# A decoder block in FP32: five instead of four steps by seven products in FFN blocks 3 to 10, and 28 instead of 20 weight sum sets

## The chip, the cores and the metric

The kernel runs on one core of a Trainium2 chip. The metric is the device time of one execution in microseconds (us), lower is better. The kernel before takes 1686.55 us, the median of three runs (1684.89 to 1690.86).

## The reference

One layer of a decoder block on 256 positions of width 2048, all in float32. Cut to what is computed:

```python
a = rmsnorm(h, norm_mix_pre)
proj = a @ w_in                                    # (2048, 17408)
q_a, k_a, v_a, q_r, f_r, i_r, g_r, gate_a, gate_r = split_columns(proj)
attn = ...       # 3 groups of 8 heads, rotary, dilated windows, outputs mixed by their denominators
r_out = ...      # HGRN2 gated linear recurrence, 8 heads, per-head RMSNorm, times silu(g_r)
y = sigmoid(gate_a) * (attn @ w_attn_branch) + sigmoid(gate_r) * (r_out @ w_hgrn_branch)
h = h + rmsnorm(y @ w_mix_out, norm_mix_post)
a = rmsnorm(h, norm_ffn_pre)
gt, up = jnp.split(a @ w_ffn_gate_up, [D_FF], axis=-1)     # D_FF = 5632
ff = (silu(gt) * up) @ w_ffn_down
h = h + rmsnorm(ff, norm_ffn_post)
```

Nearly all the arithmetic is in the products with the weights, 314 MB of them, each used once.

## The kernel before

**A product in float32.** Weights and activations are split into a high part (ScalarE copies into float32r) and a low part (VectorE subtracts). Each product of a weight tile is three matmuls: high by high, high by low, low by high.

**Items.** The program is one loop over `items` (line 669). An item is a step of a wide block (`steps`) or a chunk of a narrow one (`chunks`). Items 0 to 79 are the ten wide blocks on `w_in`, eight steps each. Items 80 to 175 are the chunks of the query and key blocks (n = 0 to 95), in which the recurrence and the attention run beside the products. Items 176 to 191 are chunks of the gate columns, 192 to 207 of the recurrence's output branch, 208 to 223 of the attention's branch. Items 224 to 239 are the mixing product, then come eleven FFN blocks (gate and up columns together, eight steps each) and two blocks of the down product.

**A wide step** multiplies four weight tiles of 128 x 512 (two row tiles k by two column groups g, 1 MB in all) by both halves of the positions: eight products, 24 matmuls. Where the block's order says so, the same 2 x 2 x 2 product is made **by seven** products (Strassen's scheme as Winograd wrote it), 21 matmuls. This needs sums of the activations (`pair_sums`, kept in `h7` for the FFN) and four sums of the weight tiles. In the orders of lines 39 to 47 each pair is (row pair m, way): 0 is plain, 1 is by seven with the weight sums made by VectorE in the step itself (lines 443 to 449), 2 is by seven with sums made long before and kept in HBM.

**The weight sums made before** come from `weight_sums` (line 296): GpSimd issues DMAs that copy tiles inside HBM and DMAs that add onto them. One set is eight DMAs of 256 KB. The generator goes forward one pass at a time from `ahead_of_time` (line 338): a pass first copies one column of the weights of item i + 3 (`beats`), so it waits until they have landed. A set of 20 jobs takes 184 passes. Before, there is a pass in each odd wide step from item 12 and in every chunk. A way 2 step loads one sum in place of a tile (line 283) and three more, 768 KB, into `sum` (line 336).

**What sets the order.** Each engine works in the order in which the program issues. For item i the loop issues `prepare(i)` (the split of item i + 2, the sums of i + 4, the loads up to three raw buffers beyond, on SP's queue), the matmuls, one pass of each lane (recurrence, attention), the evacuations, and `ahead_of_time`. The raw buffers hold 1 MB each and there are 3; there are 3 buffers for `w` and `wl`, 4 for `dh` and `dl` (two by-seven steps). `gather_first` and `gather_second` (lines 510 to 530) add the seven products' banks together after the last by-seven step of a block. A block's four result banks come from one PSUM pool and its banks of partial products from the other; `flip` says which way round.

**Around the attention.** `evac_rope` (line 920) applies the rotary factors with VectorE. `recurrence` (line 1023) works in six levels, each with matmuls, a predicated copy out of PSUM and three multiplications on VectorE. `attention` (line 948) takes the heads one after the other. All these share a ring of 17 buffers of 512 KB (`fslot`). `make_room` (line 1587) ends that phase at item 210.

Of the kernel before, what the change touches and what calls it, by code (L numbers as in the profile page):

```python
# [14 lines left out]
F32 = mybir.dt.float32  # L15
# [6 lines left out]
P = 128  # L22
# [21 lines left out]
]  # L44
GATE_UP3 = [(3, 0), (4, 0), (0, 2), (5, 0), (1, 1), (6, 0), (2, 2), (7, 0)]
GATE_UP4 = [(4, 0), (5, 0), (0, 2), (6, 0), (1, 1), (2, 2), (3, 1), (7, 0)]
DOWN = [[(m, m in by7) for m in range(KF // 2)] for by7 in (range(4, 20, 3), (2, 4, 7, 10, 13, 16, 18))]

N_F, N_RAW, N_SPLIT, AHEAD, WARM, BRIDGE = 17, 3, 3, 2, 8, 6


# [49 lines left out]
def tile_hybrid_block(ctx: ExitStack, tc: tile.TileContext, t, out):  # L101
# [194 lines left out]
    def weight_sums(jobs):  # L296
# [25 lines left out]
        for at in range(len(jobs) + 3):  # L322
# [5 lines left out]
            yield  # L328
            yield

    def fetch_sums(i):
        if i < len(items) and items[i][0] is steps:
            n = items[i][1]
            if n in pre:
                pre_in[n] = sum_slot()
                nc.sync.dma_start(pre_in[n], pre[n][:, 512:])

    def ahead_of_time(i):

        if back and (items[i][0] is chunks or i % 2):  # L340
            ahead = items[i + 3][0][items[i + 3][1]][2]
            nc.gpsimd.tensor_copy(beats, ahead[:, :1])  # L342
            advance(back)

    def split(i):
# [211 lines left out]
    def pair_sums(src, out, slot, pairs=H7):  # L557

        for m in pairs:
            f = ptile("f").rearrange("p (k t) -> p k t", k=2)  # L560
            x = src.slots[m]
            nc.vector.tensor_add(f, x[:, :, 0, :].bitcast(F32), x[:, :, 1, :].bitcast(F32))
            dst = slot().rearrange("p (z n t) -> p z n t", z=2, n=4)
            yield
            for part in seven_sums(f, dst):
                yield
                part()
            out[m] = sums_of(dst)
            yield
# [95 lines left out]
        return row[:, None, :].to_broadcast([P, n, S])  # L665

    evacs, turns, lanes, queue = deque(), deque(), [deque(), deque()], deque()
    back, turned, hold, gathers = deque(), deque(), [False], []
    ready = set()

    def advance(q):
# [248 lines left out]
    def evac_rope(key, tab, then=None):  # L920

        cos = tabs[:, tab, :]
        sin = tabs[:, tab + 1, :]

        def ev(i, src):
            if i == 0:
                qkT[key] = fslot("qk").rearrange("p (h t) -> p h t", h=4)
            yield
            w = ptile("w").rearrange("p (h t) -> p h t", h=2)
            for o, n in ((0, 64), (64, 0)):  # L930
                nc.scalar.activation(w[o : o + 64], src[n : n + 64], AF.Copy)
            yield
            u = src
            nc.vector.tensor_mul(u, src, by_rows(cos, 2))  # L934
            nc.vector.tensor_mul(w, w, by_rows(sin, 2))  # L935
            nc.vector.tensor_add(
                qkT[key][:, 2 * i : 2 * i + 2, :].rearrange("p h (two j) -> p h two j", two=2),
                u.rearrange("p h (j two) -> p h two j", two=2),
                w.rearrange("p h (j two) -> p h two j", two=2),
            )  # L940
            if i == 1 and then:
                then()
        return ev
# [79 lines left out]
    def recurrence(half):  # L1023
# [61 lines left out]
        for lev, w in enumerate(LEVELS):  # L1085
            rows = P - w if w > 8 else P
            ps = aux() if w > 1 else added(0)
            beat[0] = tick[0]
            for e in range(8) if w > 1 else ():
                es = slice(e * P, (e + 1) * P)  # L1090
                mm(
                    spans(ps[:rows, e * 64 : (e + 1) * 64], w), kk[:, e * P : e * P + rows],
                    spans(q[:, es], 2 * w)[:, :, w:], True, True,
                )
            yield
            if w < 32:
                nc.vector.copy_predicated(
                    at[:rows].rearrange("p (e n w) -> p e n w", e=8, w=2 * w)[:, :, :, w:],
                    lmask[:rows, lev, :].rearrange("p (n w) -> p n w", w=w)[:, None, :, :]
                    .to_broadcast([rows, 8, 64 // w, w]).bitcast(I32),  # L1100
                    ps[:rows].rearrange("p (e n w) -> p e n w", e=8, w=w),
                )
            for n in range(2) if w == 32 else ():
                nc.scalar.activation(
                    at[64 * n : 64 * n + 32].rearrange("p (e n w) -> p e n w", e=8, w=w)[:, :, 2 * n + 1, :],
                    ps[64 * n : 64 * n + 32].rearrange("p (e n w) -> p e n w", e=8, w=w)[:, :, n, :],
                    AF.Copy,
                )
            n = 1024 // (2 * w)
            end = spans(end, 2)  # L1110
            for x, l, r in ((kk, slice(0, w), 1), (q, slice(w, 2 * w), 0)):
                y = spans(x, 2 * w)[:, :, l]
                nc.vector.tensor_mul(y, y, end[:, :, r : r + 1].to_broadcast([P, n, w]))
            new = ends[:, used : used + n]
            used += n
            nc.vector.tensor_mul(new, end[:, :, 0], end[:, :, 1])
            end = new
            if w == 8 and half == 0:
                nc.scalar.preload_act_table_set("natural_log_exp_and_others")
            yield  # L1120
            yield
        qe, ke = (x.rearrange("p (e c t) -> p e c t", e=8, c=2) for x in (q, kk))
        ps = aux()
# [248 lines left out]
    def more_h(c):  # L1372
        if c + 1 < KD // 2:
            transpose_in(h_t, colg[:, 16:32], hT[0], c + 1)
        if c == 3:
            mix_gain(3, 1, wides[last_mix])
            residual_of(6, (0, 1), False)
            residual_of(7, (0, 1), False)
            lanes[0].append(second_norm())
        if c == 4:  # L1380
            lanes[1].append(pair_sums(hT[0], h7, lambda: rslot("so"), range(4)))

    def second_norm():
        ss, s2 = small("ss"), small("s2")
# [202 lines left out]
    def make_room(c):  # L1587
        if c == 2:
            flush(evacs)
            end_phase1()  # L1590

    early = [
# [47 lines left out]
    add_wide_block(w, (0, FF), PLAIN, lambda k: hT[0](k), None, evac_first, True, mid=more_h)  # L1640
    spare = wides[-1], 0
    for j in range(1, 11):
        add_wide_block(w, (512 * j, FF + 512 * j), GATE_UP4 if j > 1 else GATE_UP3, lambda k: hT[0](k),
                       lambda m: h7[m], evac_ffn, j % 2 == 0,
                       pre=begin_wides if j == 1 else None, turn=1)
    for j in range(2):
        add_wide_block(t["w_ffn_down"][0], (1024 * j, 1024 * j + 512), DOWN[j], act,
                       lambda m: a7[m], evac_down, j % 2 == 0, prep=prep_act,
                       pre=begin_down if j == 0 else None, turn=3 if j == 0 else None)

    wides[len(early) - 1].pre = lambda: turned.append(turned_inputs())
    wides[-3].post = lambda c: fetch_act(c // 2) if c in (1, 3) else None
    back.append(
        weight_sums([n for n, (b, i, *_) in enumerate(steps) if b.order[i][1] == 2])
    )

    load_x(0, 0, 256)
    load_wide(0, ((0, (0,)), (0, (1,))))
# [10 lines left out]
    for i in range(len(items)):  # L1669
# [13 lines left out]
            continue  # L1683
        if not (wide and b.mid):
            prepare(i)
        gather_second()
        if i >= len(items) - 3:
            continue
        multiply(i)
        if not fp:  # L1690
            gather_second()
        if b.post:
            b.post(c)
        advance(evacs)
# [77 lines left out]
```

## Time and profile before

| | us |
|---|---|
| median of three runs | 1686.55 |
| profiled execution, its own time | 1685.82 |
| its span, first to last instruction | 1684.0 |
| TensorE busy | 1670.0 |
| VectorE busy | 1374.0 |
| ScalarE busy | 1003.6 |
| GpSimd busy | 207.3 |

Durations of matmuls overlap, so a matmul's rate is read from the chain of waits (so many matmuls in so many us). In a table of windows each engine has its busy time and its instructions; the last two columns are the mean busy share of the 16 DMA engines and what they moved in GB/s. A share of 1.00 means that all of them were busy.

### The profile page before, as it was taken

What the parts mean: (1) busy time and instruction counts of PE and PEld (TensorE: products, weight loads), DVE (VectorE), ACT (ScalarE), POOL (GpSimd) and SP (SyncE); (2) the same over time, 40 slices, a digit from 0 to 9 for tenths busy, and PEclk for the clock granted to TensorE, in tenths of its full rate; (3) what the DMA queues carried; (4) which work ended last, traced back from release to release, by engine and by line L of the source; (5) the groups of instructions that cost most, each with busy time, mean ns of one, the idle gap of its engine ahead of it and who ended that gap; (6) DMA issues with size and microseconds to landing.
All of it is one profiled execution on the core that took longest, in us unless ns stands there. A gap on an engine that the chain in (4) does not pass through costs nothing.

```text
span 1684.0 us, 21755 instructions
## 1 busy us (share of the span) xinstructions
PE 1670.0 (99%) x8023; PEld 1398.8 (83%) x8023; DVE 1374.0 (82%) x1433; ACT 1003.6 (60%) x1077; POOL 207.3 (12%) x358
## 2 busy tenths in 40 slices
PE   9999999999999999999999999999999999999997
PEld 7888888888888888888888888888888888888886
DVE  6988888888786877674568878898888888898987
ACT  6666555555555545555545547666766666665653
POOL 0010101111443333232321000000000000000000
PEclk9999999999999999999999999999999999999999
DMA  8667878789999998989988656998888888888673
GB/s 293 212 215 261 257 247 246 255 258 260 271 251 265 253 249 223 226 227 291 305 215 281 214 173 200 288 272 265 286 272 270 283 263 282 271 279 273 225 266 115
DMA packets 258283, 423.47 MB, mean 251 GB/s; under 512 B 46800, under 2 KB 97152, under 8 KB 258176
## 3 DMA queue, kind: packets, MB, share of 16 engines
q1 hardware_dynamic: 231728, 360.83, 66.8%
q0 software_dynamic: 17984, 41.97, 13.2%
q10 hardware_dynamic: 8464, 19.28, 3.1%
q8 instruction: 63, 1.03, 0.3%
q14 instruction: 44, 0.36, 0.1%
HBM read 397.89 MB, written 58.20 MB: 271 GB/s over the span
## 4 chain that ended last, share of the span: by engine, by line
PE 95%; DVE 2%; DMA 1%; ACT 1%; issue 0%; DVEq 0%; ACTq 0%; SPq 0%
PE acc L138 58%; PE aux L138 36%; DMA raw<-in_w_in 1%; DVE w L380 1%; PE aux L987 0%; ACT w L379 0%; DVE wl L434 0%; PE aux L630 0%; DVE fz L1548 0%; ACT w L432 0%; DVE e L535 0%; ACT junk L1502 0%; PE aux L617 0%; DVE w L935 0%; DVE sum L934 0%
## 5 line engine op out<-in xcount | busy, mean ns | idle before, releaser
L434 DVE TENSOR_TENSOR wl<-raw,w 128x2048 fp32r<-128x2048 f32 (+1 forms) x150 | 327.2, 2188 | 87.8 <-ACT w L432 87.0
L432 ACT ACTIVATE w<-raw 128x2048 fp32r<-128x2048 f32 (+1 forms) x150 | 273.8, 1833 | 110.0 <-PE acc L138 32.8
L380 DVE TENSOR_TENSOR w<-raw,w 128x1024 fp32r<-128x1024 f32 x144 | 175.9, 1222 | 132.4 <-ACT w L379 132.4
L138 PE MATMUL acc<-xT,w 128*128 128x512 f32 (+1 forms) x1536 | 277.0, 339 | 0.2 <-DVE w L380 0.2
L138 PEld LDWEIGHTS acc<-xT,w 128*128 128x128 f32 x1536 | 235.3, 189 | 34.1 <-DVE w L380 0.6
L379 ACT ACTIVATE w<-raw 128x1024 fp32r<-128x1024 f32 x144 | 152.2, 1058 | 158.7 <-PE acc L138 115.7
L454 DVE TENSOR_TENSOR wl<-raw,w 128x2048 fp32r<-128x2048 f32 x83 | 190.0, 2290 | 31.3 <-ACT w L439 20.9
L138 PE MATMUL acc<-w,xT 128*128 128x512 f32 x694 | 207.1, 391 | 0.0
L342 POOL COPY beats<-raw 128x1 f32<-128x1 f32 x185 | 97.6, 528 | 722.9 <-DMA raw<-in_w_in 581.9
L138 PE MATMUL acc<-w,hT 128*128 128x512 f32 x510 | 166.7, 391 | 0.4 <-DVE hT L1302 0.4
L442 ACT ACTIVATE w<-raw 128x1536 fp32r<-128x1536 f32 x63 | 93.9, 1490 | 100.6 <-PE acc L138 40.3
L138 PEld LDWEIGHTS acc<-w,xT 128*128 128x128 f32 x694 | 129.8, 188 | 26.7
L456 DVE TENSOR_TENSOR dl<-sum,dh 128x1536 fp32r<-128x1536 f32 x83 | 145.3, 1751 | 1.7 <-ACT dh L452 1.7
L138 PE MATMUL aux<-w,xT 128*128 128x512 f32 x454 | 144.9, 389 | 0.0
L138 PE MATMUL aux<-w,hT 128*128 128x512 f32 x414 | 134.6, 389 | 0.0
L452 ACT ACTIVATE dh<-sum 128x1536 fp32r<-128x1536 f32 x83 | 123.4, 1487 | 10.7 <-PE acc L138 3.3
L138 PEld LDWEIGHTS acc<-w,hT 128*128 128x128 f32 x510 | 95.7, 188 | 20.5 <-DVE hT L1302 0.9
L138 PEld LDWEIGHTS aux<-w,xT 128*128 128x128 f32 x454 | 85.2, 188 | 17.7
L138 PE MATMUL acc<-wl,hT 128*128 128x512 f32 x255 | 99.3, 389 | 0.0
L138 PE MATMUL acc<-wl,xT 128*128 128x512 f32 x251 | 97.7, 389 | 0.0
L138 PEld LDWEIGHTS aux<-w,hT 128*128 128x128 f32 x414 | 77.7, 188 | 16.1
L138 PE MATMUL acc<-w,a 128*128 128x512 f32 x282 | 89.2, 389 | 0.2 <-DVE e L535 0.2
(282 smaller groups left out, 3029.3 us busy)
## 6 DMA issues: line engine op xcount, KB each, us to landing
raw<-in_w_in SPq DMA_DIRECT2D x270, 512.0 KB, 5.8
raw<-in_w_ffn_gate_up SPq DMA_DIRECT2D x156, 512.0 KB, 5.5
raw<-in_w_ffn_down SPq DMA_DIRECT2D x88, 512.0 KB, 5.4
presum<-in_w_ffn_gate_up POOLq DMA_DIRECT2D x120, 256.0 KB, 7.3
raw<-in_w_mix_out SPq DMA_DIRECT2D x32, 512.0 KB, 5.0
sum<-presum SPq DMA_DIRECT2D x20, 768.0 KB, 6.7
act<-acts SPq DMA_DIRECT2D x22, 512.0 KB, 6.8
presum<-presum POOLq DMA_DIRECT2D x40, 256.0 KB, 6.4
```

The costliest lines, as they stand in the source:

```text
L138: nc.tensor.matmul(ps, lhsT, rhs, start=start, stop=stop, skip_group_check=True)
L342: nc.gpsimd.tensor_copy(beats, ahead[:, :1])
L379: nc.scalar.activation(wh, raw, AF.Copy)
L380: nc.vector.tensor_sub(wl, raw, wh.bitcast(F32))
L432: nc.scalar.activation(hi[:, c], raw[:, c], AF.Copy)
L434: nc.vector.tensor_sub(lo[:, c], raw[:, c], hi[:, c].bitcast(F32))
L442: nc.scalar.activation(hi[:, 512:], raw[:, 512:], AF.Copy)
L452: nc.scalar.activation(high, sums, AF.Copy)
L454: nc.vector.tensor_sub(lo, raw, hi.bitcast(F32))
L456: nc.vector.tensor_sub(low, sums, high.bitcast(F32))
```

## The change

FFN blocks 3 to 10 take a new order, `GATE_UP5`: three plain steps, three of way 2 and two of way 1, where `GATE_UP4` had four, two and two. `pair_sums` makes the activation sums of row pair 4 as well. This asks for 28 sets of weight sums: GpSimd makes the first 20 as before, the other 8 are made by `weight_sums_beside`. It loads four tiles by SP's queue into two ring buffers, lets VectorE add four times and stores the set by ScalarE's queue. Two such generators run, from items 177 and 181, seven passes to a set, one pass per item; `make_room` empties them. GpSimd's passes come in every wide step, in two of three chunks up to n = 127 and in each chunk after it. Moved are: the three multiplications of each recurrence level (ahead of the predicated copy, in a pass of their own), a pass in `evac_rope`, and `gather_second` (directly after the item's matmuls). The two down blocks swap their PSUM pools.

```diff
+GATE_UP5 = [(5, 0), (6, 0), (0, 2), (2, 2), (1, 1), (4, 2), (3, 1), (7, 0)]
+SPARSE = 128
+N_SUMS, BESIDE = 20, 177
...
+    def weight_sums_beside(jobs):
+        for n in jobs:
+            x = [fslot("pre") for _ in range(2)]
+            b, i = steps[n][:2]
+            m = b.order[i][0]
+            r = [x[g][:, c * 512 : (c + 1) * 512] for g, c in ((0, 1), (0, 0), (1, 0), (1, 1))]
+            for q, (g, k) in enumerate(product(range(2), repeat=2)):
+                rows = slice((2 * m + k) * P, (2 * m + k + 1) * P)
+                nc.sync.dma_start(r[q], b.w[rows, b.cols[g] : b.cols[g] + 512])
+            for _ in range(3):
+                yield
+            for to, by in ((2, 0), (0, 1), (1, 2), (3, 1)):
+                nc.vector.tensor_add(r[to], r[to], r[by])
+                if by:
+                    yield
+            pre[n] = dram.tile([P, 2048], F32, name=nm("presum"))
+            for g in range(2):
+                nc.scalar.dma_start(pre[n][:, g * 1024 : (g + 1) * 1024], x[g])
+            yield
...
     def ahead_of_time(i):
-        if back and (items[i][0] is chunks or i % 2):
+        for n, q in enumerate(beside):
+            if i >= BESIDE + 4 * n:
+                advance(q)
+        kind, n = items[i][:2]
+        if back and (kind is steps or n >= SPARSE or n % 3):
             ahead = items[i + 3][0][items[i + 3][1]][2]
-            nc.gpsimd.tensor_copy(beats, ahead[:, :1])
+            nc.gpsimd.tensor_copy(beats, ahead[:, 1023:1024])
             advance(back)
...
     def pair_sums(src, out, slot, pairs=H7):
         for m in pairs:
+            for _ in range(8 if m == 4 else 0):
+                yield
...
     # evac_rope, between the multiplications and the addition
+            if not then:
+                yield
...
     # recurrence, each level: these lines now stand ahead of the predicated copy
+            for x, l, r in ((kk, slice(0, w), 1), (q, slice(w, 2 * w), 0)):
+                y = spans(x, 2 * w)[:, :, l]
+                nc.vector.tensor_mul(y, y, end[:, :, r : r + 1].to_broadcast([P, n, w]))
+            new = ends[:, used : used + n]
+            nc.vector.tensor_mul(new, end[:, :, 0], end[:, :, 1])
+            yield
...
-            lanes[1].append(pair_sums(hT[0], h7, lambda: rslot("so"), range(4)))
+            lanes[1].append(pair_sums(hT[0], h7, lambda: rslot("so"), range(5)))
...
     def make_room(c):
         if c == 2:
             flush(evacs)
+            for q in beside:
+                flush(q)
             end_phase1()
...
-        add_wide_block(w, (512 * j, FF + 512 * j), GATE_UP4 if j > 1 else GATE_UP3, lambda k: hT[0](k),
+        add_wide_block(w, (512 * j, FF + 512 * j), (None, GATE_UP3, GATE_UP4)[j] if j < 3 else GATE_UP5, lambda k: hT[0](k),
...
-                       lambda m: a7[m], evac_down, j % 2 == 0, prep=prep_act,
+                       lambda m: a7[m], evac_down, j % 2 == 1, prep=prep_act,
...
+    back.append(weight_sums(kept[:N_SUMS]))
+    for n, q in enumerate(beside):
+        q.append(weight_sums_beside(kept[N_SUMS + n :: 2]))
...
-        gather_second()
         if i >= len(items) - 3:
             continue
         multiply(i)
-        if not fp:
-            gather_second()
+        gather_second()
```

More of the change, by code (lines that the diff above doesn't have):

```diff
@@ L667, in tile_hybrid_block @@
     evacs, turns, lanes, queue = deque(), deque(), [deque(), deque()], deque()
-    back, turned, hold, gathers = deque(), deque(), [False], []
+    back, beside, turned, hold, gathers = deque(), (deque(), deque()), deque(), [False], []
     ready = set()
@@ L1095, in recurrence @@
             yield
+            n = 1024 // (2 * w)
+            end = spans(end, 2)
+            for x, l, r in ((kk, slice(0, w), 1), (q, slice(w, 2 * w), 0)):
+                y = spans(x, 2 * w)[:, :, l]
+                nc.vector.tensor_mul(y, y, end[:, :, r : r + 1].to_broadcast([P, n, w]))
+            new = ends[:, used : used + n]
+            used += n
+            nc.vector.tensor_mul(new, end[:, :, 0], end[:, :, 1])
+            end = new
+            yield
             if w < 32:
@@ L1108, in recurrence @@
                 )
[L1109 to L1117, printed above, removed]
             if w == 8 and half == 0:
                 nc.scalar.preload_act_table_set("natural_log_exp_and_others")
-            yield
             yield
@@ L1652, in tile_hybrid_block @@
     wides[-3].post = lambda c: fetch_act(c // 2) if c in (1, 3) else None
-    back.append(
-        weight_sums([n for n, (b, i, *_) in enumerate(steps) if b.order[i][1] == 2])
-    )
+    kept = [n for n, (b, i, *_) in enumerate(steps) if b.order[i][1] == 2]
+    back.append(weight_sums(kept[:N_SUMS]))
+    for n, q in enumerate(beside):
+        q.append(weight_sums_beside(kept[N_SUMS + n :: 2]))
     load_x(0, 0, 256)
```

## The prediction, made before the changed kernel was run

> **What bounds the kernel now.** I read the page's first part, then the windows by stage, then the chain of waits.
>
> ```profile
> span 1684.0 us, 21755 instructions
> PE 1670.0 (99%) x8023; PEld 1398.8 (83%) x8023; DVE 1374.0 (82%) x1433; ACT 1003.6 (60%) x1077; POOL 207.3 (12%) x358
> ```
>
> ```profile
> core 0: us, PE busy (x) PEld busy (x) DVE busy (x) ACT busy (x) POOL busy (x), PEclk, DMA share, GB/s
> 67.00:428.00 361.00, 361.00 (x1594) 298.94 (x1593) 310.42 (x241) 209.20 (x172) 43.73 (x63) 1.00 0.79 249
> 428.00:545.00 117.00, 117.00 (x724) 103.37 (x723) 91.56 (x127) 67.31 (x95) 44.59 (x75) 1.00 1.00 259
> 545.00:585.00 40.00, 39.84 (x231) 34.44 (x230) 30.06 (x47) 24.24 (x42) 14.50 (x28) 1.00 1.01 258
> 585.00:610.00 25.00, 22.92 (x139) 20.21 (x138) 19.92 (x28) 11.28 (x17) 9.42 (x17) 0.99 1.02 254
> 610.00:750.00 140.00, 139.82 (x876) 124.20 (x876) 98.12 (x157) 74.30 (x126) 41.21 (x77) 0.99 0.90 226
> 750.00:860.00 110.00, 110.00 (x557) 93.44 (x556) 58.79 (x83) 56.85 (x76) 34.69 (x65) 1.00 1.00 279
> 1117.00:1443.00 326.00, 326.00 (x1440) 270.04 (x1439) 287.74 (x211) 221.23 (x170) 0.00 (x0) 1.00 0.88 274
> ```
>
> TensorE sets the time: it is idle for 14.0 us of 1684.0, and its granted clock is 0.99 to 1.00. So fewer matmuls are worth their full time if nothing else becomes late. What could is to be seen in the last columns. From 428 to 610 us and again from 750 to 860 us the DMA engines are full (share 1.00 to 1.02) and TensorE still hardly waits. In the FFN stretch, which is blocks 3 to 10, VectorE is 88% busy and the DMA engines 88%.
>
> **The matmuls saved.**
>
> ```profile
> 944.41 11.56 PE aux L138 x51
> ```
>
> A matmul takes 11.56 / 51 = 0.227 us in this piece of the chain. A plain step is 24 of them, 5.44 us, one by seven 21, 4.76 us. Eight blocks change one step each: 24 matmuls, **-5.4 us**.
>
> **What the extra step costs in the FFN.** Rows of the FFN stretch alone (groups of instructions, window 1117 to 1443):
>
> ```profile
> L454 DVE TENSOR_TENSOR wl<-raw,w 128x2048 fp32r<-128x2048 f32 x32 | 73.3, 2290 | 25.7 <-ACT w L439 16.0 <-ACT w L450 9.7
> L434 DVE TENSOR_TENSOR wl<-raw,w 128x2048 fp32r<-128x2048 f32 x32 | 72.6, 2287 | 8.1 <-ACT w L432 8.0
> L456 DVE TENSOR_TENSOR dl<-sum,dh 128x1536 fp32r<-128x1536 f32 x32 | 56.0, 1751 | 1.7 <-ACT dh L452 1.7
> L452 ACT ACTIVATE dh<-sum 128x1536 fp32r<-128x1536 f32 x32 | 47.4, 1481 | 6.6 <-PE acc L138 3.3 <-PE aux L138 2.4
> L443 DVE TENSOR_TENSOR sum<-raw 128x1024 f32<-128x1024 f32 x16 | 19.5, 1216 | 0.0
> L448 DVE TENSOR_TENSOR raw<-raw,sum 128x512 f32<-128x512 f32 x16 | 11.1, 692 | 0.5
> ```
>
> A block takes 180 x 0.227 = 40.8 us now and 40.1 us after. VectorE has 287.74 / 8 = 36.0 us of work in it; one `dl` of 1.75 us comes on top: 37.7 of 40.1, 94%. ScalarE goes from 27.7 to 29.1 us. The average fits, but the five by-seven steps now stand in a row. A step of way 2 needs 2.29 + 1.75 = 4.04 us of VectorE, one of way 1 also the three sums (1.22 + 2 x 0.69), 6.6 us: five steps need 3 x 4.04 + 2 x 6.6 = 25.4 us while TensorE takes 5 x 4.76 = 23.8 us. So VectorE loses 1.6 us of its lead over TensorE in them, where before three in a row cost 4.04 + 2 x 6.6 - 3 x 4.76 = 3.0 us after a plain step had given it time (5.44 - 2.29 = 3.2 us). Worse is the buffer: there are four `dh`/`dl`, two steps' worth, so ScalarE's `dh` of step k + 2 can't begin before TensorE ends step k; the rows show such waits already (6.6 us for 32). Behind it in ScalarE's order stand the next high part and the transposed activations. Bounds: nothing, if the lead lasts, and 1 us a block, if each run of five ends with TensorE waiting. I take 0.2 us a block, **+1.6 us**, near the lower end since the average has 2.4 us to spare a block. The load of 768 KB more a block adds about 2.5 us of DMA time (priced below) to 0.88 x 40.8 = 35.9: 38.4 of 40.1 us, covered by the three raw buffers loaded ahead.
>
> `gather_second` comes 1 to 2 us earlier in VectorE's order. There it waits for the seventh product, and behind it waits the low part of the item after next, which needs its `w` buffer from the same step anyway: nothing. Row pair 4's activation sums are fewer than eight VectorE operations of at most 0.7 us each, spread by eight passes: nothing, since their use lies blocks later; uncovered they would be under 5 us once.
>
> **The down blocks' banks.**
>
> ```profile
> 1442.83 0.70 DVE e L535
> 1443.67 22.73 PE acc L138 x99
> ```
>
> The last FFN block and the first down block use the same pool now, so TensorE waits for the addition that frees a bank. The swap takes that away. It can be worth nothing, if TensorE had just come, or the addition's whole 0.70 us; I take the middle, **-0.4 us**.
>
> **Passes and order around the attention.** The page's queues price a DMA:
>
> ```profile
> q1 hardware_dynamic: 231728, 360.83, 66.8%
> q0 software_dynamic: 17984, 41.97, 13.2%
> q10 hardware_dynamic: 8464, 19.28, 3.1%
> ```
>
> Shares are of 1684 us of all 16 engines. SP's queue (q1): 1125 us for 360.83 MB, 3.12 us a MB. ScalarE's (q10): 2.71 us a MB. GpSimd's (q0): 222 us in 184 passes, 1.21 us a pass. Before there are 34 passes up to item 79 and 96 in items 80 to 175; after it is 68 and 64. So 34 x 1.21 = 41 us of DMA time move into 67 to 428 us, whose share rises from 0.79 to 0.90: nothing, covered by the loads ahead; if that cover fails, a few us. And 39 us leave the stretch 428 to 750, whose share falls from about 0.96 to 0.84.
>
> ```profile
> 601.87 1.31 DVE L1097 COPY_PREDICATED at<-lmask,aux 128x512 f32<-128x512 int32 x1
> 602.98 0.72 DVE L1113 TENSOR_TENSOR kk<-kk,f 128x512 f32<-128x512 f32 x1
> 603.62 0.68 DVE L1113 TENSOR_TENSOR q<-q,f 128x512 f32<-128x512 f32 x1
> 604.22 0.68 DVE L1116 TENSOR_TENSOR end<-f 128x512 f32<-128x512 f32 x1
> ```
>
> These four VectorE operations in a row, with the rotary's three ahead, stand before the split at 607 us, and TensorE loses 25.00 - 22.92 = 2.1 us there. The edits put passes between them, and late loads are fewer. I take **-2.2 us**, all idle time of 428 to 610; the bounds are -2.4 and, if the copy that is now later holds its PSUM bank too long, +2.
>
> **The eight sets of `weight_sums_beside`.** They run in items 177 to 210.
>
> ```profile
> 747.85 8.21 PE acc L138 x36
> 838.89 8.18 PE acc L138 x36
> 848.85 24.50 PE acc L138 x108
> ```
>
> A chunk there has 12 matmuls in `acc`. Item 176 is the first at 747.85, item 206 the first at 848.85: items 177 to 210 are 750 to 860 us, the window with DMA share 1.00. What is added: 8 x 1.05 MB of loads on SP's queue, 8.39 x 3.12 = 26.2 us, and as much of stores on ScalarE's, 8.39 x 2.71 = 22.7 us. What goes: 10 of 34 passes, 12.1 us. Net 36.8 us of DMA time into 110 us that have none free.
>
> ```profile
> 772.00:792.00 20.00, 20.00 (x106) 17.10 (x105) 9.08 (x14) 12.58 (x16) 5.70 (x12) 1.00 1.04 334
> raw<-in_w_hgrn_branch SPq DMA_DIRECT2D x16, 512.0 KB, 8.8
> gate<-waits SPq DMA_DIRECT2D x6, 512.0 KB, 12.6
> 555.52 16.83 DMA raw<-in_w_in x2
> ```
>
> The fullest 20 us have a share of 1.04, so at most some 3 us of 110 are still to be had: 33.5 us too much. Not all of it reaches TensorE. Weights land 8.8 us after their issue here, and in the chain at 555.52 it took 16.8 us until ScalarE waited for them: landings may grow by 8 us first. And GpSimd's passes can be put off, since each waits for the weights of three items on and their sums are used far later: 24 passes are 29 us of DMA time, I let 12 us of them slide. That leaves 33.5 - 8 - 12 = **+13.5 us**. Bounds: 0, if all passes slide and the loads spread, and 25.5 us, if none does. I take the middle, as no row has such a load for so long: the one burst at 555.52 (1.5 MB beside the weights) cost TensorE at most the 2.2 us above.
>
> VectorE's part, 32 additions of 0.69 us, 22 us, fits: 58.8 + 22 of 110 us. But it waits in order: three items, 10 us, after the issue of the loads, with the splits' low parts behind. At 8.8 us to landing that holds, beyond 10 us each set delays the splits and so the raw buffers. It is in the 13.5.
>
> The Trainium skill, DMA: Bandwidth & Descriptors, section Where 436 GB/s comes from, gives a ceiling of 435 GB/s for the 16 engines together. My demand by bytes is 279 + 153 - 21 = 411 GB/s and would fit below it, and then this term would be near nothing, as in the first rival. No window here goes above 334 GB/s in this stage.
>
> **Sum.** 1685.8 - 5.4 + 1.6 - 0.4 - 2.2 + 13.5 = 1692.9, told as **1693 us**. It is made against the profiled execution's own 1685.82 us (span 1684.0); the median of the runs shown, 1686.55, is 0.7 above. A difference under 0.3%, 5.1 us, is about what can't be told from no change.
>
> **Rivals.**
>
> (a) *Faster: the DMA engines take it.* The passes of GpSimd slide and the sets' loads fall into gaps between bursts. For it, from the groups of this window alone:
>
> ```profile
> L342 POOL COPY beats<-raw 128x1 f32<-128x1 f32 x33 | 13.6, 412 | 66.5 <-DMA raw<-in_w_hgrn_branch 34.2 <-DMA raw<-in_w_in 19.8 <-DMA raw<-in_w_attn_branch 12.5
> ```
>
> The passes already wait 66.5 us of these 110 for weights, so they are paced by landings, and TensorE waited nowhere in this window although the gates were loaded beside (12.6 us to landing). Against it: share 1.00. Time 1692.9 - 13.5 = 1679.4. It decides where landings of the branch weights stay under 16 us.
>
> (b) *The FFN gives it back.* VectorE and the `dh` buffers become the bound, 0.7 us a block, so that the step saves nothing: with (a), 1679.4 - 1.6 + 5.6 = 1683.4; with half of the 13.5, 1690. For it: 94% and five steps in a row. Against: a plain step before and after has VectorE catch up 3.2 us each.
>
> (c) *Much slower: the passes keep their turn.* Then 25.5 instead of 13.5 us: 1704.9. For it: GpSimd's operations wait little for each other. Against: their own wait for weights. The Trainium skill, same page, section Queues, rings and completion order, says that each engine goes round the queues that have work, packet by packet. By that the weights' queue has no precedence over the other two, as (c) needs.
>
> **Chances.** Forecast 0.40 (1686 to 1700, of which 0.08 is within 0.3%), (a) 0.37 (1676 to 1682, 0.02 of it within), (b) 0.12 (0.10 within, 0.02 slower), (c) 0.11. Faster by over 0.3%: 0.35, within: 0.08 + 0.02 + 0.10 = 0.20, slower: 0.32 + 0.02 + 0.11 = 0.45. Cases of both signs hold most, so the range for 8 in 10 goes from 1676 to 1704; the likeliest one's own is 1686 to 1700.
>
> **What would show it.** Saved matmuls: the FFN blocks 3 to 10 at 40.1 us each with TensorE never idle; a wait of TensorE for `dl` or `wl`, or ScalarE's `dh` waiting longer than 6.6 us, speaks for (b). The window 750 to 860: its work, found by its items, takes 13 us longer, with ScalarE's L379 waiting for branch weights and VectorE for the sets' loads; with no such waits it is (a). The idle 2.1 us near 606 gone, DMA share down to 0.85 there. The 0.7 us of L535 at the first down block gone. I am wrong if TensorE waits in the early wide blocks, where I cost the 41 us of DMA time at nothing.

## The result and the profile after

| | us | ratio to before, with 95% interval |
|---|---|---|
| before, median | 1686.55 | |
| after, median of five runs | 1713.28 (1711.62 to 1715.19) | 1.0155 [1.0141, 1.0169] |
| after, profiled execution | 1712.13, span 1710.4 | |

The change makes the kernel slower by 1.55%. From the page of the kernel after, its first and third parts (busy time and instructions of each engine; queues with packets, MB and their share of the 16 DMA engines):

```profile
span 1710.4 us, 21891 instructions
PE 1673.9 (98%) x7999; PEld 1397.7 (82%) x7999; DVE 1405.9 (82%) x1479; ACT 1012.1 (59%) x1086; POOL 227.9 (13%) x358
q1 hardware_dynamic: 237616, 375.51, 68.3%
q0 software_dynamic: 17984, 41.97, 11.9%
q10 hardware_dynamic: 10768, 27.67, 4.6%
```

TensorE has 24 matmuls fewer, as meant, yet it is idle for 36.5 us where it was idle for 14.0. GpSimd's queue moves the same bytes; SP's moves 14.7 MB more (eight sets of 1.05 MB to sum and 6.3 MB of finished sums for the FFN), ScalarE's 8.4 MB more.

The stages are best compared by items, since they lie at other times. A stage lasts from its first matmul to the first matmul of the next; the table has its length after less its length before, in the profiled executions:

| stage | after less before, us |
|---|---|
| items 0 to 79 | +0.72 |
| 80 to 175 | -2.23 |
| 176 to 191 | **+15.42** |
| 192 to 207 | **+17.76** |
| 208 to 223 | +0.65 |
| mixing | 0.00 |
| FFN blocks | -5.82 |
| down blocks and end | -0.10 |
| all | +26.40 |

Everything that was meant to gain has gained, and 33.8 us are lost where the eight sets are summed. The windows by stage of the kernel after (columns as in the table of before; 750 to 905 us are items 177 to about 214, 1149 to 1470 us the FFN blocks 3 to 10):

```profile
67.00:428.00 361.00, 361.00 (x1594) 299.01 (x1593) 306.54 (x236) 209.96 (x172) 92.46 (x127) 1.00 0.90 267
585.00:610.00 25.00, 24.95 (x150) 21.92 (x149) 21.79 (x31) 13.20 (x19) 4.53 (x8) 1.00 0.83 222
750.00:860.00 110.00, 94.24 (x441) 77.49 (x439) 59.52 (x92) 45.39 (x62) 17.07 (x33) 0.91 0.96 308
860.00:905.00 45.00, 37.53 (x169) 30.44 (x168) 24.97 (x33) 13.46 (x16) 8.52 (x17) 0.92 0.94 287
1149.00:1470.00 321.00, 321.00 (x1418) 265.81 (x1417) 297.48 (x219) 230.34 (x178) 0.00 (x0) 1.00 0.94 297
```

The wide stage takes a share of 0.90 without a wait, the 2 us lost near 606 are saved, and the FFN blocks never wait. In 750 to 905 us TensorE is idle for 15.76 + 7.47 = 23.2 us, at a granted clock of 0.91 and 0.92. The DMA share there is 0.96 and 0.94, below the 1.00 of before: the engines are *less* full in the stage that loses. So a full DMA system alone doesn't explain it. The view of waits for 744 to 890 us (engine, what waits, for what: us in total, times, longest) names the one that was late; its last line is from the view of the DMA queue's own waits:

```profile
POOL beats L370 <- DMA raw<-in_w_hgrn_branch: 60.1, 9, 12.0
DVE pre L347 <- DMA pre<-in_w_ffn_gate_up: 50.5, 7, 12.6
...
PEld acc L141 <- DVE w L408: 24.7, 5, 7.6
...
SPq L273 <- DVE w L408: 69.2, 13, 13.1
```

VectorE waits 50.5 us, in 7 of the 8 sets, for the loads of the set. TensorE then waits for the low parts (L408) that stand behind on VectorE. And SP waits 69.2 us for the same low parts before it may load the next weights (L273) into their buffers, with the next set's loads behind it. ScalarE waits only 1.2 us for weights of the recurrence's branch, though the prediction named such waits as the sign of its own mechanism.

SP's wait by itself is no sign of a loss. In the kernel before, where TensorE lost nothing here, it was longer (746 to 856 us; L270 and L380 are the same two lines):

```profile
SPq L270 <- DVE w L380: 94.5, 18, 8.1
```

There SP had filled all buffers and waited for the next free one. What is new is that VectorE, which frees them, itself waits for loads that SP issues behind the weights. The chain of waits of the kernel after has it in this order (start, length, what; L273 are SP's weight loads, L343 those of the sets):

```profile
850.92 1.23 DVE w L408
852.20 0.37 SPq L273
852.61 0.56 SPq L273
853.22 0.47 SPq L343
853.73 0.43 SPq L343
854.20 14.78 DMA pre<-in_w_ffn_gate_up
869.00 0.70 DVE pre L347
869.73 0.69 DVE pre L347
870.42 1.15 DVE w L408
871.61 4.31 PE acc L141 x11
```

This is a circle: a low part frees a buffer, SP issues weights and set loads, VectorE stands at L347 until they have landed, and only then makes the next low part. The last line holds a second cost: 11 matmuls take 4.31 us, 0.39 us each in place of 0.227.

### The profile page after: what moved, and what is told of

Its sections match the earlier page's. It is cut to its first block, busy times and chain, and to the rows that moved or that the text cites. A ratio compares the mean times of both kernels' runs of the same rounds, so it can differ in the third digit from the quotient of the medians.

```text
span 1710.4 us, 21891 instructions
## 1 busy us (share of the span) xinstructions
PE 1673.9 (98%) x7999; PEld 1397.7 (82%) x7999; DVE 1405.9 (82%) x1479; ACT 1012.1 (59%) x1086; POOL 227.9 (13%) x358
## 3 DMA queue, kind: packets, MB, share of 16 engines
q0 software_dynamic: 17984, 41.97, 11.9%
## 4 chain that ended last, share of the span: by engine, by line
PE 88%; DMA 6%; DVE 3%; ACT 1%; issue 1%; SPq 0%; POOL 0%; DVEq 0%; ACTq 0%; POOLq 0%
PE acc L141 52%; PE aux L141 35%; DMA pre<-in_w_ffn_gate_up 3%; DMA raw<-in_w_in 1%; DVE w L408 1%; DMA v<-waits 1%; DMA presum<-pre 1%; ACT w L407 0%; DVE pre L347 0%; DVE wl L462 0%; DMA x<-in_x 0%; DVE fz L1580 0%; PE aux L660 0%; ACT w L460 0%; SPq L273 0%
## 5 line engine op out<-in xcount | busy, mean ns | idle before, releaser
L462 DVE TENSOR_TENSOR wl<-raw,w 128x2048 fp32r<-128x2048 f32 (+1 forms) x142 | 308.9, 2183 | 76.1 <-ACT w L460 75.2
L460 ACT ACTIVATE w<-raw 128x2048 fp32r<-128x2048 f32 (+1 forms) x142 | 258.6, 1828 | 113.9 <-PE aux L141 28.1
L408 DVE TENSOR_TENSOR w<-raw,w 128x1024 fp32r<-128x1024 f32 x144 | 176.2, 1224 | 96.1 <-ACT w L407 95.9
L482 DVE TENSOR_TENSOR wl<-raw,w 128x2048 fp32r<-128x2048 f32 x91 | 208.4, 2290 | 25.2 <-ACT w L467 20.8
L370 POOL COPY beats<-raw 128x1 f32<-128x1 f32 x185 | 119.3, 645 | 791.3 <-DMA raw<-in_w_in 584.2
L141 PE MATMUL acc<-w,xT 128*128 128x512 f32 x694 | 211.5, 398 | 10.6 <-DVE w L408 10.6
L484 DVE TENSOR_TENSOR dl<-sum,dh 128x1536 fp32r<-128x1536 f32 x91 | 159.5, 1753 | 0.0
L141 PE MATMUL acc<-w,hT 128*128 128x512 f32 x462 | 153.2, 391 | 0.4 <-DVE hT L1334 0.4
L480 ACT ACTIVATE dh<-sum 128x1536 fp32r<-128x1536 f32 x91 | 135.3, 1486 | 14.2 <-PE acc L141 4.2
L141 PE MATMUL aux<-w,hT 128*128 128x512 f32 x366 | 121.1, 389 | 0.0
L141 PEld LDWEIGHTS aux<-w,xT 128*128 128x128 f32 x454 | 85.2, 188 | 17.7
L141 PE MATMUL aux<-w,a 128*128 128x512 f32 x282 | 89.1, 389 | 0.0
L478 ACT ACTIVATE w<-raw 128x512 fp32r<-128x512 f32 x63 | 39.7, 631 | 83.0 <-DVE raw L476 83.0
```

The source lines that it names most:

```text
L141: nc.tensor.matmul(ps, lhsT, rhs, start=start, stop=stop, skip_group_check=True)
L370: nc.gpsimd.tensor_copy(beats, ahead[:, 1023:1024])
L408: nc.vector.tensor_sub(wl, raw, wh.bitcast(F32))
L460: nc.scalar.activation(hi[:, c], raw[:, c], AF.Copy)
L462: nc.vector.tensor_sub(lo[:, c], raw[:, c], hi[:, c].bitcast(F32))
L478: nc.scalar.activation(hi[:, :512], raw[:, :512], AF.Copy)
```

## The experiments

Theory V: VectorE's wait in order for loads that were issued only three items before. Theory D: more DMA work than the stage has room for, as the prediction had it. Rival of both for the rest: the moved passes and the moved order cost something elsewhere. Each run is compared by items as above; the medians are those of its timed executions.

| kernel | median us | ratio to before | lost in items 176 to 223, us | mixing | FFN blocks |
|---|---|---|---|---|---|
| after | 1713.28 | 1.0155 [1.0141, 1.0169] | 33.8 | 0.0 | -5.8 |
| e1: no additions | 1699.4 (two of four) | 1.0081 [1.0061, 1.0102] | 17.8 | 0.0 | -5.7 |
| e2: additions later | 1695.47 | 1.0057 [1.0042, 1.0072] | 18.9 | 0.0 | -5.9 |
| e3: four sets | 1693.17 | 1.0043 [1.0027, 1.0058] | 7.1 | +4.1 | -1.8 |
| e4: all by GpSimd | 1687.12 | 1.0009 [0.9991, 1.0027] | 0.0 | +11.7 | -4.5 |
| e5: only the moves | 1683.76 | 0.9989 [0.9979, 0.9998] | 0.0 | 0.0 | -0.4 |
| e6: as e4, none in the mixing | 1691.66 | 1.0033 [1.0015, 1.0051] | 0.0 | +5.2 | +2.9 |
| e7: as e2, no GpSimd passes there | 1683.99 | 0.9987 [0.9975, 0.9998] | 0.0 | +2.3 | -4.6 |
| e8: after, no GpSimd passes there | 1694.44 | 1.0054 [1.0030, 1.0077] | 14.1 | +7.5 | -4.5 |
| e9: as e7, passes earlier | 1680.15 | 0.9959 [0.9944, 0.9974] | 0.0 | 0.0 | -5.9 |
| e10: as e9, fewer of them | 1684.07 | 0.9978 [0.9964, 0.9993] | 0.0 | +1.4 | -5.8 |
| e11: as e8, additions at once | 1695.61 | 1.0059 [1.0038, 1.0080] | 13.7 | +2.8 | -5.1 |

The stage columns are from one profiled execution each, for e1 that of 1696.71 us; that of e4 (1695.14 us) lay near the top of its ten, that of e6 (1695.79) was the longest of its six, that of e8 (1706.25) was the longest of its ten and lost another 4.2 us before item 80, that of e7 (1680.68) 3.3 us below its median, and that of e10 (1680.05) was the shortest of its twelve.

**e1: VectorE's additions taken out.** The sets are loaded, nothing is added, and other data of the same size is stored, so the sums of these eight sets aren't made.

```diff
-            for to, by in ((2, 0), (0, 1), (1, 2), (3, 1)):
-                nc.vector.tensor_add(r[to], r[to], r[by])
-                if by:
-                    yield
+            for by in (1, 2, 1):
+                yield
...
-                nc.scalar.dma_start(pre[n][:, ...], x[g])
+                nc.scalar.dma_start(pre[n][:, ...], tabs.rearrange("p a c -> p (a c)"))
```

> The eight sets' loads (8.4 MB) and stores (8.4 MB) stay at their places and on their queues, but VectorE's 32 additions are left out and the stores take their data from a table that has long been there, so the stored sums are not the weights' sums. Theory V (VectorE waits in its order for loads issued three items before; the changed kernel's trace has 50.5 us of such waits): no engine waits for the loads any more, TensorE's 33.2 us lost in items 176 to 208 go down to a few us, about 1680 us. Theory D (the DMA engines have more work than time, as I predicted, 33.5 us too much of it): the same bytes still delay the branch weights, 1695 to 1712 us, with ScalarE waiting for weights in that stage.

Measured: the loss falls from 33.8 to 17.8 us and moves, 14.3 us of it to items 192 to 207 and 3.4 us to the 16 behind them. Two of four timed executions took 1696.71 and 1702.11 us, as theory D had it; the two others took 1848.91 and 4349.53, stay unexplained and are left out of the median. The window of the loss in e1, its waits, and one of the DMA queue's own waits there:

```profile
797.00:867.00 70.00, 61.57 (x288) 50.64 (x287) 29.07 (x43) 28.02 (x39) 8.57 (x20) 0.93 1.04 343
```

```profile
ACT w L405 <- DMA pre<-in_w_ffn_gate_up: 14.1, 2, 9.3
ACT w L405 <- DMA raw<-in_w_hgrn_branch: 12.2, 5, 5.2
...
SPq L343 <- DMA raw<-in_w_hgrn_branch: 18.1, 6, 7.3
```

Here the DMA engines *are* full, 1.04, and it is ScalarE that waits: for branch weights (`raw`) and, as the profile names it, for the sets' loads, though nothing on ScalarE reads these in e1. So both theories hold a part: without VectorE's wait half of the loss stays, and it has the mark of D. SP too waits for earlier loads to land before it can issue the next. How much of the loss is engine time and how much SP's order, no run here separates; none loads the sets from another queue.

**e2: the additions two items later,** all four in one item, so a set takes as many items as before.

```diff
-            for _ in range(3):
+            for _ in range(5):
                 yield
             for to, by in ((2, 0), (0, 1), (1, 2), (3, 1)):
                 nc.vector.tensor_add(r[to], r[to], r[by])
-                if by:
-                    yield
+            yield
```

> The same work, but the additions stand five items after their loads instead of three, all four in one pass, so that a set still takes seven passes. At 3.4 us an item VectorE would then wait only where a landing takes over 17 us (the changed kernel's loads landed after 8.7 us median, 16.2 at most). V: most of the 33 us come back, 1680 to 1690 us, and VectorE's waits for the loads fall from 50.5 us to under 15. D: the bytes are the same, so it stays above 1700 us.

Measured: 18.9 us lost, with all the work done, in the same place as in e1, and a time between the two expectations. The first 16 items lose nothing where after lost 15.4. But VectorE's waits for the loads don't fall under 15 us as expected; they are 18.8 us, so e2 isn't free of V. Of e2, the window, VectorE's waits (744 to 880 us), and GpSimd's passes over these items (by tile `beats`: duration, first and last start):

```profile
797.00:867.00 70.00, 57.27 (x271) 47.07 (x271) 42.26 (x61) 27.41 (x39) 12.57 (x21) 0.93 1.04 346
```

```profile
DVE pre L347 <- DMA pre<-in_w_ffn_gate_up: 18.8, 6, 6.7
```

```profile
L369 POOL COPY beats<-raw x22: 183/606/1258, 748.8 to 876.7; 128x1 f32<-128x1 f32 x22
```

22 of the 24 planned passes still ran in the stage. They did not slide away.

**e3: four sets beside, not eight** (GpSimd makes 24).

```diff
-N_SUMS, BESIDE = 20, 177
+N_SUMS, BESIDE = 24, 177
...
-    for n, q in enumerate(beside):
-        q.append(weight_sums_beside(kept[N_SUMS + n :: 2]))
+    beside[0].append(weight_sums_beside(kept[N_SUMS:]))
```

> One generator with four sets instead of two with eight; GpSimd makes 24 sets, its last passes in the first FFN blocks. D: 24.5 us of DMA time are added to items 177 to 210 and 12 us taken by the thinner passes, which the loads ahead and the free share nearly take: 0 to 4 us lost there. V: half of the waits of the changed kernel's first part, 5 to 10 us. Total 1681 to 1692 us.

Measured: 7.1 us lost there, about a fifth of 33.8 but more than the 0 to 4 us expected, with VectorE's wait at a quarter (the waits of e3, 744 to 890 us):

```profile
DVE pre L347 <- DMA pre<-in_w_ffn_gate_up: 12.5, 3, 6.5
```

New is a loss elsewhere: GpSimd's 32 more passes end later, and the mixing and the FFN blocks give 8.1 us back, so the time misses its range too, by 1.2 us.

**e4: no set beside; GpSimd makes all 28,** a pass in every item.

```diff
-N_SUMS, BESIDE = 20, 177
+N_SUMS, BESIDE = 28, 177
...
-        if back and (kind is steps or n >= SPARSE or n % 3):
+        if back:
```

> All 28 sets by GpSimd, with a pass in every item from 12 on; nothing by VectorE. V and D both: the 33 us are gone. The rest of the change is then seen alone: 5.8 us less in the FFN, and the attention stage as before or up to 2 us better, about 1679 to 1683 us. If the passes in every chunk bring the DMA engines back to a share of 1.0 in 428 to 610 us, the idle 2 us there come back too.

Measured: nothing lost in items 176 to 223, but 1687.12 us where 1679 to 1683 were expected. The passes now run on into the mixing, which loses 11.7 us in the profiled execution, and items 80 to 175 lose 0.8 us where after gained 2.2. Two pieces of the chain of waits in the mixing:

```profile
901.09 16.23 DMA raw<-in_w_mix_out
...
981.21 9.17 DMA raw<-in_w_ffn_gate_up
```

**e5: only the moves** (the order of the FFN blocks and its sums as before; the pace of the passes, the attention's order, `gather_second` and the banks as after).

```diff
-... (None, GATE_UP3, GATE_UP4)[j] if j < 3 else GATE_UP5 ...
+... GATE_UP4 if j > 1 else GATE_UP3 ...
...
-            lanes[1].append(pair_sums(hT[0], h7, lambda: rslot("so"), range(5)))
+            lanes[1].append(pair_sums(hT[0], h7, lambda: rslot("so"), range(4)))
```

> FFN orders as before the change (20 sets, all by GpSimd, none by VectorE); the passes in other items, the moves in the recurrence, the rotary step and the gathering, and the swapped banks stay. V and D both: 1686 less the 2.2 us of the attention stage and about 0.1 to 0.4 us of the banks, about 1683 to 1685 us; over 1690 would say that the moves cost something that the ledger by stages doesn't show.

Measured: +0.73 us in items 0 to 79, -3.40 in 80 to 175 and -0.38 in the FFN blocks, -3.17 in all. The windows of e5:

```profile
585.00:610.00 25.00, 24.96 (x151) 21.96 (x150) 21.80 (x33) 12.43 (x19) 5.29 (x9) 1.00 0.83 248
...
750.00:860.00 110.00, 110.00 (x557) 93.40 (x557) 59.17 (x84) 55.38 (x73) 26.59 (x47) 1.00 0.85 249
```

The moves alone are a small gain, and they make room in 750 to 860 us (share 0.85).

**e6: as e4, with no passes in the mixing product.**

```diff
-N_SUMS, BESIDE = 20, 177
+N_SUMS, BESIDE = 28, 177
...
-        if back and (kind is steps or n >= SPARSE or n % 3):
+        if back and not 224 <= i < 240:
```

> All 28 sets by GpSimd, a pass in every item but those of the mixing product (224 to 239), where e4's profiled run lost 11.7 us beside the loads of inputs and gains; 36 passes are left for the FFN's first blocks. Theory: e4's missing gain and its spread (1683 to 1696 us) come from that stage. Then 1679 to 1683 us with a smaller spread. If it stays at 1687 us, the passes in every chunk or those in the FFN take the gain.

Measured: slower, not faster. The passes put off go on in the FFN, which loses 8.7 us against after's FFN; and the mixing still loses 5.2, where ScalarE waits for a reload of the input (waits of e6, 898 to 1010 us). So the passes in the mixing are not the whole of the 11.7 us that e4 lost there. Why this load was late was not tried further.

```profile
ACT w L460 <- DMA hx<-in_x: 9.8, 1, 9.8
```

**e7 and e8: no GpSimd pass in items 177 to 210,** e7 with e2's later additions, e8 with the additions of after. Together with after and e2 they are a two by two table of the two causes.

```diff
-        if back and (kind is steps or n >= SPARSE or n % 3):
+        if back and not 177 <= i < 211 and (kind is steps or n >= SPARSE or n % 3):
```

> As e2 (additions five items after their loads), and GpSimd makes no pass in items 177 to 210; the 24 passes left out there come at the end, in the first FFN blocks. e1 and e2 both lost 14 to 18 us in items 192 to 208 with the DMA engines at a share of 1.04, without or with the waits of VectorE, so theory D holds for that part. D: 24 passes of 1.2 us are 29 us of DMA time taken out of that stage, so the loss of e2 there, 18 us, falls to under 5 us and the total to 1678 to 1684 us. If it stays above 1690 us, the bytes beside the weights are not what delays them there.

> The changed kernel with its additions three items after the loads, and no pass of GpSimd in items 177 to 210. V and D together: D's part (about 15 us, as between e2 and the kernel with both) goes, V's stays as far as landings take longer than the three items; VectorE's waits for the loads are over 15 us and the time 1685 to 1698 us. D alone: 1680 us, as e7. V alone: it stays at 1713 us.

| lost in items 176 to 223 | 24 passes beside | none |
|---|---|---|
| additions three items behind | 33.8 (after) | 14.1 (e8) |
| five items behind | 18.9 (e2) | 0.0 (e7) |

The two causes nearly add up: 14.1 + 18.9 = 33.0. The medians of the whole runs add up less well: later additions save 17.8 us with the passes and 10.5 without, leaving out the passes saves 18.8 and 11.5. Each cause is clear in them too, but how far the two add is not settled, as the stages of e8 are those of its longest execution. They also share a path. In after, part of what the passes cost comes by way of VectorE: without them (e8) its waits are 35.0 us instead of 50.5, and the longest landing of a set's load is 10.4 us instead of 16.2.

In e8 the DMA engines aren't full (share 0.87 from 750 to 860 us) and VectorE's wait is there all the same; in e7 all loads and stores of the eight sets fit. Of e8 the wait, of e7 the window:

```profile
DVE pre L347 <- DMA pre<-in_w_ffn_gate_up: 35.0, 6, 9.0
```

```profile
750.00:860.00 110.00, 110.00 (x558) 93.40 (x557) 79.71 (x116) 55.03 (x73) 3.46 (x6) 1.00 0.97 351
```

351 GB/s for 110 us with TensorE never idle. So it isn't the sets' loads and stores alone that are too much, but these and GpSimd's passes.

**e11: e8 with the additions at once,** to see whether the lead or the spread over four items is what costs. The stores come later, so that a set is as long.

```diff
                 nc.vector.tensor_add(r[to], r[to], r[by])
-                if by:
-                    yield
+            for _ in range(3):
+                yield
```

> The kernel after without a GpSimd pass in items 177 to 210, and with a set's four additions in one item, still three items behind its loads; the stores come three items later, so a set takes the same number of items. It differs from the run without passes only in the grouping of the additions, and from the run that lost nothing in these items only in the lead of three items in place of five. Theory (the lead decides: VectorE comes to the first addition before the data have landed, and all behind it is late): items 176 to 208 still lose 6 to 14 us, with 20 to 35 us of VectorE waits for the loads. Rival (it was the splitting over four items, with a wait possible in each, or the place of the stores): 0 to 2 us lost there and under 8 us of such waits.

Measured: 13.7 us lost, 29.3 us of VectorE's waits; the lead decides. How long a lead is can be read from the timeline (start, length, what; in brackets the idle time before and its end). The second set of e11, and of e7:

```profile
765.77 4.34 SPq L343 DMA_DIRECT2D pre<-in_w_ffn_gate_up  x4
...
777.89 0.69 DVE L347 TENSOR_TENSOR pre<-pre,pre 128x512 f32<-128x512 f32 x1 [5.10 <-DMA pre<-in_w_ffn_gate_up]
```

```profile
764.35 4.36 SPq L343 DMA_DIRECT2D pre<-in_w_ffn_gate_up  x4
...
778.84 0.68 DVE L347 TENSOR_TENSOR pre<-pre,pre 128x512 f32<-128x512 f32 x1
```

In e11 VectorE stood ready at 777.89 - 5.10 = 772.79, 7.0 us after SP began to issue. SP took 4.34 us to issue the four loads. With five items the addition came 14.5 us after the first issue and did not wait. The loads themselves take 7.3 us in the median of e7, 10.5 at most, each from its own issue (view by tile):

```profile
DMA to landing us min/median/max: 5.0/7.3/10.5
```

The lead doesn't stay at 7 us. The third set of e11:

```profile
781.92 1.11 SPq L273 DMA_DIRECT2D raw<-in_w_hgrn_branch  x2
783.08 2.69 SPq L343 DMA_DIRECT2D pre<-in_w_ffn_gate_up  x4
...
791.04 0.69 DVE L347 TENSOR_TENSOR pre<-pre,pre 128x512 f32<-128x512 f32 x1 [6.87 <-DMA pre<-in_w_ffn_gate_up]
```

VectorE stood ready 791.04 - 6.87 - 783.08 = 1.1 us after the first issue. SP had been held up by the weights at 781.92, whose buffer a low part of VectorE (780.76 to 781.91 in the chain) freed only then, behind the additions that had waited until 777.89. Worked out in this way, the leads of e11's eight sets are 7.5, 7.0, 1.1, 1.8, 10.5, 4.1, 6.9 and 3.4 us, those of e7's 10.4 to 14.5 us (five items of 3.4 us, as e2's expectation reckoned, would be 17), with 1.5 us of waits in one set. So one late addition can shorten the leads of the sets behind it.

**e9 and e10: e7 with earlier passes.** The late passes of e7 ran on until 1141 us. In e9 every chunk up to 95 has a pass (the edit against e7 is shown), in e10 seven of eight.

```diff
-        if back and not 177 <= i < 211 and (kind is steps or n >= SPARSE or n % 3):
+        if back and not 177 <= i < 211:
```

> The kernel with the additions two items later and no GpSimd pass in items 177 to 210 (the run that lost nothing in those items, but 2.3 us in the mixing and 1.2 of the 5.8 us in the FFN blocks, where its late passes ran on until 1141 us), now with a pass in every chunk up to 95 in place of two of three, so 32 passes come earlier. Theory (late passes are what costs there): the mixing at +0 to +0.5 us against the kernel before, blocks 3 to 10 at -5.5 to -5.8, so about 8.5 us below the kernel before in all by the stages, 1677 to 1681 us. Rival (the full DMA engines of 428 to 610 us take it back): items 80 to 175 lose the 2.8 us that they had gained and the time stays at 1683 to 1685.

> As the run with a pass in every chunk up to 95, but one chunk of eight is left out, so 20 passes come earlier and about 12 more run after the attention. Theory (late passes cost, each by what it meets in the mixing): mixing at +0 to +1.5 us, blocks 3 to 10 at -5.5, 1678 to 1682 us. Rival (the time goes by the passes in the full stretch 428 to 610): this is 0.5 to 1 us faster than the run with every chunk, since it puts fewer there.

Measured: e9 takes 1680.15 us, 0.41% less than before, the fastest of all here: the mixing back at 0.0, the FFN blocks at -5.9, and items 80 to 175 at -0.8 instead of e7's -2.8. So the theory holds and the rival has a part. Of e9 the passes that are left after 890 us:

```profile
L369 POOL COPY beats<-raw x9: 183/779/2242, 894.1 to 934.2; 128x1 f32<-128x1 f32 x9
```

e10 was expected at 1678 to 1682 us. Its profiled execution lies there, its median is 2.1 us above that range and 3.9 above e9. The trace, of its shortest execution, shows only the mixing's 1.4; what the others lose was not seen.

## Why the prediction was wrong

The direction and the place were right, the time was not: 1693 was told, 1713.28 came, above the range's 1704. With a chance of 0.45 for slower, the direction alone says little.

**Saved matmuls, -5.4: right.** The FFN blocks gain 5.82 us. The bank's 0.4 lies just ahead of the first down matmul and so in this sum; e5, which saves no matmul, has -0.38 there. 5.82 - 0.38 = 5.44.

**The extra step in the FFN, +1.6: nothing.** TensorE is busy for 321.00 of 321.00 us. From the groups of the kernel after in that window:

```profile
L484 DVE TENSOR_TENSOR dl<-sum,dh 128x1536 fp32r<-128x1536 f32 x40 | 70.1, 1753 | 0.0
L480 ACT ACTIVATE dh<-sum 128x1536 fp32r<-128x1536 f32 x40 | 59.3, 1482 | 9.9 <-PE acc L141 4.2 <-PE aux L141 3.9 <-DVE sum L477 1.1
```

ScalarE's `dh` waits 9.9 us for 40, as it waited 6.6 for 32: the same 0.2 us each. VectorE's lead outlasts the five steps, as the lower bound had it.

**The down blocks' bank, -0.4, and the 2.2 us near 606: right.** Items 80 to 175 gain 2.23 us in after and 3.40 in e5. **The passes in the wide stage:** nothing was told, and nothing clear is seen. Items 0 to 79 change by +0.7 us in after and by -0.3 to +0.8 in the other runs, which all have the same passes there, but for the one execution of e8.

**The eight sets, +13.5: this term failed, in two places.** The prediction put 33.5 us too much of DMA work into the stage, of which 8 were to go into longer landings and 12 into passes that slide. (A slip of the sum: a share of 1.04 for 110 us is 4.4 us more, not 3.) The DMA work without VectorE's additions cost 17.8 us (e1); e2's 18.9 still holds some of VectorE's waits. So far the mechanism was right and the size 4 to 5 us low. The passes didn't slide (22 of 24 ran), and the weights' landings (by tile `raw`, from 744 us to the end of the stage) grew from 8.3 us in the median before to 9.5 (e1) and 10.6 (e2), not by 8 us. What absorbed the other 13 us or so of the 33.5 the runs don't show.

The step that was wrong is the sentence on VectorE: "three items, 10 us, after the issue of the loads ... At 8.8 us to landing that holds ... It is in the 13.5." It did not hold and was not in it. Without a full DMA system, e8 and e11 lose 14.1 and 13.7 us by this wait alone, and with five items for three it is gone (e7). Three items are 10 us of TensorE's time. But the lead runs from SP's issue, and SP issues in order, behind weights whose buffers VectorE must free; four loads took it 4.34 us in e11's second set and 9.52 in that of after:

```profile
765.98 9.52 SPq L343 DMA_DIRECT2D pre<-in_w_ffn_gate_up  x4
...
783.59 0.69 DVE L347 TENSOR_TENSOR pre<-pre,pre 128x512 f32<-128x512 f32 x1 [9.86 <-DMA pre<-in_w_ffn_gate_up]
```

VectorE came to this addition 783.59 - 9.86 - 765.98 = 7.8 us after the first issue, before the last of the four loads was issued. In the next two sets of after it came 2.5 and 3.6 us after the first issue. A landing time of 8.8 us can't be met by that. The prediction named the queue behind the wait (the splits, then the raw buffers) rightly but gave it no price of its own.

**The rivals.** (a), 1679.4, came true for a version that isn't the change: e9's 1680.15, with the passes out of the way and a longer lead. Its ground did not carry it: the passes are paced by landings (in e2 GpSimd waits 54.3 us for the recurrence's weights alone), but they run in the stage all the same, and without them e2's 18.9 us are gone (e7). (b) did not happen. (c), 25.5 us of DMA work, was too high for that work, and its time, 1704.9, is the nearest for another reason: e1 shows D at 17.8, and V was in no rival.

## What to carry to other kernels

Measure the lead of a load from its issue to the moment when the consuming engine gets to the instruction, not in time of the engine that sets the pace: here three items were 10 us for TensorE, but 7 to 8 us from the *first* of four issues to VectorE's arrival in the first two sets, and down to 1.1 us in later ones. An engine that waits in order costs everything that stands behind it, and if the freed buffers feed the loads it waits for, the delay carries over to the sets that follow; price it apart from a shortage of DMA time. Work that may be done at any time belongs where the DMA engines have room: leaving 24 passes out beside the sets took 18.9 us away (e2 and e7), where the mixing lost 11.7 us with passes and 5.2 without (e4 and e6, one execution each), and 34 more in the wide stage cost nothing that stands out.

## What was not expected of the hardware

**A short idle time of TensorE halves its clock.** Four stretches of 6.8 us in the kernel after have a granted clock of 0.50 (windows; the clock is the third column from the end):

```profile
782.80:789.60 6.80, 3.40 (x8) 2.73 (x9) 5.98 (x7) 0.00 (x0) 1.36 (x2) 0.50 0.58 162
803.30:810.10 6.80, 5.23 (x12) 3.67 (x13) 5.41 (x12) 3.41 (x6) 0.18 (x1) 0.50 0.74 283
851.10:857.90 6.80, 5.71 (x13) 4.45 (x14) 5.48 (x10) 2.79 (x6) 2.73 (x6) 0.50 1.04 373
868.20:875.00 6.80, 3.39 (x8) 2.74 (x9) 5.96 (x8) 0.00 (x0) 0.49 (x1) 0.50 0.49 174
```

They belong to the four longest idle times of TensorE there, 4.53 to 7.22 us; the first of them in the timeline (in brackets the idle time before):

```profile
786.20 4.38 PE L141 MATMUL acc<-w,xT 128*128 128x512 f32 x11 [5.56 <-DVE w L408]
```

The clock falls at 782.8 us, 2.2 us after TensorE went idle at 780.64, and 3.4 to 3.8 us after it in the other three; the matmuls behind the gap go at half speed. In the four, TensorE is busy for 17.7 us, and half of that, 8.9 us, is lost beside the 23.2 us of idle time in 750 to 905 us: 32.1 of the 33.8 us. The Trainium skill, TensorE: Matmul & The Clock Gate, Part 1, says that a monitor of the array's recent activity switches its clock between half and full; the trace agrees, with 0.50 for 6.8 us at a time.

How long the idle time must be can be narrowed down. Within each trace here, the changes of the granted clock between 60 us and the last 15 us lie on a grid of 3.41 us. Where TensorE at full clock was idle for 2.01 us or more of one interval of this grid (18 times in the traces of all 13 kernels), the clock fell to 0.50 at its end; where it was idle for 1.87 us or less, it did not. So the 2.08 us near 607 us in the kernel before halved the clock, and an idle time of 2.67 us in e2 (861.20 to 863.87 us), which the grid cuts in two, did not.

**The DMA share is not a rate.** The engines were full at 259 GB/s in 428 to 545 us of before (share 1.00), at 346 GB/s in e2's 70 us (1.04), and had room at 351 GB/s in e7 (0.97). By the queues' shares before, 256 KB (0.262 MB) cost 0.82 us of all engines on SP's queue (3.12 us a MB) and 222 / 41.97 x 0.262 = 1.39 us on GpSimd's, whose DMAs copy and add inside HBM. At 1.21 us a pass, 24 passes are 29 us of all engines.
